# Attention of a diffusion backbone: whole steps, a fused table add and row maximum, and chunks placed between the transposes of the probabilities and their products

## The chip, the cores and the metric

The kernel runs on one core of a Trainium2 chip. The metric is the device time of one execution in microseconds (us). A core has a matrix engine (TensorE, PE in the profile; the loading of its weights is a row of its own, PEld), a vector engine (VectorE, DVE), a scalar engine for functions and copies (ScalarE, ACT), a general engine (GpSimd, POOL) and a queue that issues most transfers (SyncE, SP). Matrix products land in PSUM, eight banks of 128 partitions by 512 numbers of 32 bits; all else lies in SBUF.

## The reference

Two layers over 256 latent tokens of width 1024, with 256 context tokens beside them. Each layer is a half-step gated network, a mixer, and another half-step. The mixer of the first layer is the attention that the change touches:

```python
qkv = (hx @ w_qkv).reshape(B, S, 3, N_HEADS, HEAD_DIM)
q = apply_axial_rope(qkv[:, :, 0], rope)
k = apply_axial_rope(qkv[:, :, 1], rope)
v = qkv[:, :, 2]
...
s_win = jnp.einsum('bjqhd,bjkhd->bhjqk', q_r, k_blk).astype(jnp.float32) * scale
s_win = jnp.where(mask, s_win + bias.astype(jnp.float32)[None], -jnp.inf)
s_ctx = jnp.einsum('bjqhd,bchd->bhjqc', q_r, k_c).astype(jnp.float32) * scale
p = jax.nn.softmax(jnp.concatenate([s_win, s_ctx], axis=-1), axis=-1).astype(v.dtype)
return (jnp.einsum('bhjqk,bjkhd->bjqhd', p[..., :nk], v_blk)
        + jnp.einsum('bhjqc,bchd->bjqhd', p[..., nk:], v_c))
```

The latent tokens are a grid of 4 rows by 64 columns, and there are 16 heads of 64. Every latent query sees all four rows, a window of 16 columns of them with a table of biases per head, and all 256 context keys, in one softmax. So for one head and 128 queries the kernel has a row of 512 scores: 256 latent keys, to which a table of bias and mask is added, and 256 context keys without one.

## The kernel before

All weights stream once from memory. To keep 32-bit accuracy on fast products, every operand is split into a high part (ACT copies it rounded) and a low part (DVE subtracts): `split`, lines 104 to 106, for activations and lines 178 to 181 for weights. One *chunk* is six products of 512 columns (`mmu`, lines 152 to 159).

PE's instructions run in the order in which the code writes them. For the other engines a planner orders the instructions by priority when the kernel is built; `tc.high_priority(offset=n)` moves a group ahead.

Attention is the loop at lines 902 to 930. Before it the first half of the queries (`q_half(0)`) and the first quarter of keys and values (`kv_quarter(0)`) are computed. The rest is a *filler*, which the loop draws chunk by chunk between its own work: `kv_quarter` 1 and 2 (16 chunks each), `q_half(1)` (8 chunks, queries of heads 8 to 15), `kv_quarter(3)` (16 chunks). When it is used up, the output projection (`last_filler`, weights `wo`) follows as filler with nine chunks; its last chunks need the last heads.

A step of two heads and one half `qt` of the queries consists of:

- `scores` (lines 804 to 826): products into two banks S of the PSUM tag "at" (three banks); then per head, on DVE, the table add on the first 256 columns (L818) and the negated row maximum over 512 (L820), on ACT the exponential with its row sum (L822), on DVE the reciprocal (L823), on ACT the scaling (L824);
- `probs_T` (lines 830 to 837) per head: four transposes on PE into a bank of the tag "tp" (two banks), PT, then the split into pT;
- `values` (lines 841 to 861) per head, after both halves of the queries: eight products of 256 columns into a bank of the tag "mm" (three banks), o; ACT copies one half of the partitions (L854), DVE adds the other (L855); every second head is split into oT.

The filler accumulates in "mm" banks too. The projection's order (`order_late`, lines 421 to 427) opens two "mm" banks and then one "at" bank and holds them to the end.

The loop runs over 32 half steps (a head and a query half). Scores of a pair are written at even half steps, one head is transposed two half steps later (A_LAG), its values one more half step later (V_LAG). R0 to R3 say how many chunks are drawn in a half step, half of them before the transposes. The projection starts at half step 24, which is the start of step 12. A piece of work that is due later (`Late`, lines 113 to 125) is written when its count of chunks has passed or when someone needs it: so the transposes of queries (`qT`, line 791) and keys (`kT`, line 773).

The bias table of a head is loaded column-reversed into one of four rotating tiles, POOL adds the mask (L730), and L818 reads it backwards.

Of the kernel before, what the change touches and what calls it, by code (L numbers as in the profile page):

```python
# [20 lines left out]
NH = 16  # L21
# [14 lines left out]
LEAD = 5  # L36
TAIL = 3
XAT = 1
A_LAG = 2
A_PRE = 2  # L40
NX_AT = 2
R0 = 2.4
R1 = 2.9
R2 = 1.9
R3 = 1.0
LN_LAG = (5, 5)
LT_LAG = (5, 5)
F0_LAG = (5, 5, 6, 7)
G_LAG = 4
ROPE_EARLY = 70  # L50
S_EARLY = 40
V_LAG = 1
AHEAD = 3
P_EARLY = 70
V_EARLY = 70
W_HI = 2
# [8 lines left out]
def backbone_kernel(  # L65
# [6 lines left out]
    nc = tc.nc  # L72
# [8 lines left out]
    hp = phase.__enter__()  # L81
# [6 lines left out]
    def nm(s):  # L88
        uid[0] += 1
        return f"{s}_{uid[0]}"  # L90
# [13 lines left out]
    def split(src, hi, lo):  # L104
        nc.scalar.activation(hi, src, AF.Copy)  # L105
        nc.vector.tensor_tensor(out=lo, in0=src, in1=hi.bitcast(F32), op=ALU.subtract)  # L106
# [20 lines left out]
    def settle():  # L127
        while waiting:
            waiting[0].get()
# [72 lines left out]
    warm = cp.tile([1, 1], F32, tag="warm", name="warm")  # L202
    nc.gpsimd.memset(warm, 0.0)
    nc.scalar.activation(warm, warm, AF.Silu)
    crow = cp.tile([16, P], F32, tag="crow", name="crow")
    sync.dma_start(crow[0:8], c[0].rearrange("(a b) -> a b", b=P))
    sync.dma_start(crow[8:16], c_ctx.rearrange("(a b) -> a b", b=P))
    pt = tpb("ctp")
# [172 lines left out]
    def run(gen):  # L381
        for _ in gen:
            pass
# [332 lines left out]
        return r1  # L716

    BIAS = {}

    def bias_pair(h, qt):  # L720


        for hh in (h, h + 1):
            bt = hp.tile([P, 4, 64], F32, tag="bias", bufs=4, name=nm("bias"))
            for i in range(2):
                bias_dma[:] = [sync.dma_start(bt[64 * i:64 * i + 64],
                                              bass.AP(na_rpb_rev.tensor,
                                                      na_rpb_rev.offset + hh * 465 + (7 - 2 * qt - i) * 31 - 48,
                                                      [[1, 64], [31, 4], [1, 64]]))]
            nc.gpsimd.tensor_tensor(out=bt, in0=bt, in1=win_sb[:, ::-1].unsqueeze(1).to_broadcast([P, 4, 64]),  # L730
                                    op=ALU.add)
            BIAS[hh, qt] = bt[:, :, ::-1]

    w_qkv = na_w_qkv[0]

# [16 lines left out]
    def kv_quarter(g, res):  # L752
        krs, v = [], []

        def each(t, bk):
            if t < 2:
                krs.append(roped(bk[:, 0:256], t, 1, 4))
            else:
                r1 = rtile(256)
                nc.scalar.activation(r1, bk[:, 0:256], AF.Copy)  # L760
                krs.append(r1)
            v.append(act(F32R, "v"))
            z = v[t].rearrange("p (h s d) -> p h s d", h=4, s=2)
            split(bk[:, 256:512].rearrange("p (h d) -> p h d", h=4), z[:, :, 0], z[:, :, 1])

        yield from tile_panel(D + g * 256, 2 * D + g * 256, [hTs[t] for t in range(4)], "wkv", each)

        def rest():
            kT = []
            for j in range(2):  # L770
                ps = tpb("kT")
                for t in range(4):
                    nc.tensor.transpose(ps[:, t * P:(t + 1) * P], krs[t][:, j * P:(j + 1) * P], ident)
                hi, lo = act(F32R, "kTh"), act(F32R, "kTl")
                split(ps, hi, lo)
                kT.append((hi, lo))
            return kT

        res.append((Late(1, rest), v))
# [24 lines left out]
    def scores(h, qt):  # L804

        ch = h % 8 // 2
        qh, ql = Q[h // 8].get()[ch // 2]
        qs = slice((ch % 2) * 256 + qt * P, (ch % 2) * 256 + (qt + 1) * P)
        kh, kl = KV[h // 4][0].get()[(h % 4) // 2]
        banks = [bank("at", "S") for _ in range(2)]  # L810
        for f in range(3):
            for i in range(2):
                ps = slice(64 * i, 64 * i + 64)
                nc.tensor.matmul(banks[i], (qh, qh, ql)[f][ps, qs], (kh, kl, kh)[f][ps, :], start=f == 0, stop=f == 2)
        res = []
        for i, S in enumerate(banks):
            Sv = S[:, 0:256].rearrange("p (a b) -> p a b", a=4)
            nc.vector.tensor_tensor(out=Sv, in0=Sv, in1=BIAS.pop((h + i, qt)), op=ALU.add)  # L818
            mx = hp.tile([P, 3], F32, tag="mx", bufs=6, name=nm("mx"))
            nc.vector.tensor_reduce(out=mx[:, 0:1], in_=S, axis=AX.X, op=ALU.max, negate=True)  # L820
            pr = hp.tile([P, 512], F32, tag="pr", bufs=4, name=nm("pr"))
            nc.scalar.activation(pr, S, AF.Exp, bias=mx[:, 0:1], accum_out=mx[:, 1:2])  # L822
            nc.vector.reciprocal(mx[:, 2:3], mx[:, 1:2])  # L823
            nc.scalar.activation(pr, pr, AF.Copy, scale=mx[:, 2:3])  # L824
            res.append(pr)
        return res

    PT = {}
# [57 lines left out]

    box = []
    fill = filler()
    rate = [R0] * 8 + [R1] * 8 + [R2] * 8 + [R3] * 12
    credit = 0.0  # L890
    steps = [(h + i, qt) for h in range(0, NH, 2) for qt in range(2) for i in range(2)]
    prs = {}
    LAG = A_LAG
    fin = None

    def fill_some(n):
        for _ in range(n):
            if next(fill, 0) == 0:
                break

    fill_some(A_PRE)
    for i in range(len(steps) + LAG + V_LAG):
        if i == NX_AT:
            new_x(0, 0, s2t)
            for t in range(2):
# [12 lines left out]
        if i >= 24 and fin is None:  # L918
            run(fill)
            fin = last_filler()  # L920
            fill = islice(fin, 9)
        fill_some((n + 1) // 2)
        if 0 <= i - LAG < len(steps):
            with tc.high_priority(offset=P_EARLY):
                probs_T(*steps[i - LAG], prs.pop(i - LAG))
        fill_some(n // 2)
        j = i - LAG - V_LAG
        if j >= 0 and steps[j][1] == 1:
            with tc.high_priority(offset=V_EARLY):
                values(steps[j][0])  # L930
    run(fill)
    run(fin)
    phase.__exit__(None, None, None)
# [129 lines left out]
```

## Time and profile before

| what | value |
|---|---|
| median of 3 runs | 1285.99 us (1285.16 to 1287.23) |
| profiled execution, its own time | 1289.17 us |
| span of the profiled execution, first to last instruction | 1287.4 us |
| mean granted PE clock | 0.996 |
| first scores of attention (L814) | 441.8 us from the span's start |
| last o product (L849) | 589.2 us |
| DVE over the span | 955.1 us (74%) |
| ACT over the span | 591.2 us (46%) |

The two times differ because one is a single profiled execution and the other the median of runs without a profile. A row of the profile such as `PE o L849 <- DVE pT L106` says that a product of line 849 into the tile o stood idle until the DVE instruction of line 106 had written pT. A PE row shows a product's modelled length; products are pipelined, so the distance from start to start says more about pace.

### The profile page before, as it was taken

The numbers are of one execution on the slowest core, as the hardware profiler recorded it, in microseconds if no ns is written. First come the engines' busy times: TensorE is split into PE (matmuls) and PEld (weight loads), VectorE is DVE, ScalarE is ACT, GpSimd is POOL, SyncE is SP. The second block draws the span as 40 slices with busy tenths as digits, with TensorE's granted clock in tenths as the row PEclk, the third lists the DMA queues.
The fourth block names the chain that finished last, engine by engine and source line by source line (L and its number), as shares of the span: only waits on it lengthen the run. The fifth ranks groups of instructions, "written<-read, shape, count | busy, mean of one in ns | idle before, by whom it ended". The sixth has DMA issues, their size and how long they took to land.

```text
span 1287.4 us, 17193 instructions
## 1 busy us (share of the span) xinstructions
PE 1257.7 (98%) x5890; PEld 1007.0 (78%) x5890; DVE 955.1 (74%) x1683; ACT 591.2 (46%) x1148; POOL 42.0 (3%) x71
## 2 busy tenths in 40 slices
PE   7999999999999999988999999999999999999997
PEld 4787778788778877766887787887787877788886
DVE  3699877485658777788998787757778788855545
ACT  2432132413236456686555435654435645655431
POOL 0000000000001111110000000000000000000000
PEclk9999999999999999999999999999999999999999
DMA  9977569484622744464999887666887764666641
GB/s 284 299 231 243 181 193 297 131 297 146 198 78 76 215 91 92 90 147 149 305 331 328 295 294 262 215 215 225 289 287 241 215 211 147 210 217 185 231 155 51
DMA packets 202712, 268.59 MB, mean 209 GB/s; under 512 B 30026, under 2 KB 149298, under 8 KB 202624
## 3 DMA queue, kind: packets, MB, share of 16 engines
q1 hardware_dynamic: 202624, 267.49, 65.9%
q8 instruction: 46, 0.75, 0.2%
q14 instruction: 42, 0.34, 0.1%
HBM read 265.27 MB, written 2.17 MB: 208 GB/s over the span
## 4 chain that ended last, share of the span: by engine, by line
PE 78%; DVE 8%; DMA 8%; ACT 3%; issue 2%; SPq 1%; POOL 0%; DVEq 0%; ACTq 0%
PE w L156 13%; PE w L157 13%; PE w L159 13%; PE f L541 6%; PE f L542 6%; PE f L543 6%; DMA ar<-in_ada_w_dram 5%; DMA w1r<-in_ffn_w_in_dram 2%; PE wkv L156 2%; PE wkv L157 2%; PE wkv L159 2%; PE wc L156 2%; PE wc L157 2%; PE wc L159 2%; DVE w1l L181 2%
## 5 line engine op out<-in xcount | busy, mean ns | idle before, releaser
L178 ACT ACTIVATE w1h<-w1r 128x512 fp32r<-128x512 f32 x352 | 203.3, 626 | 185.0 <-PE w L159 75.4
L181 DVE TENSOR_TENSOR w1l<-w1r,w1h 128x512 fp32r<-128x512 f32 x352 | 227.6, 684 | 66.5 <-ACT w1h L178 64.3
L156 PE MATMUL w<-w1h,hTh 128*128 128x512 f32 x528 | 211.6, 401 | 3.8 <-ACT hTh L105 3.7
L247 DVE SCALAR_TENSOR_TENSOR acc<-ar,cst,acc 128x512 f32<-128x512 f32 x266 | 187.2, 745 | 34.8 <-DMA ar<-in_ada_w_dram 34.8
L157 PE MATMUL w<-w1l,hTh 128*128 128x512 f32 x528 | 207.7, 393 | 0.0
L156 PE MATMUL w<-w2h,gh 128*128 128x512 f32 (+1 forms) x446 | 175.4, 394 | 0.0
L157 PE MATMUL w<-w2l,gh 128*128 128x512 f32 (+1 forms) x446 | 173.7, 390 | 0.3 <-DVE w2l L181 0.3
L178 ACT ACTIVATE w2h<-w2r 128x512 fp32r<-128x512 f32 x176 | 101.5, 624 | 140.9 <-PE w L159 131.6
L159 PE MATMUL w<-w1h,hTl 128*128 128x512 f32 x528 | 163.9, 392 | 0.6 <-DVE hTl L106 0.6
L181 DVE TENSOR_TENSOR w2l<-w2r,w2h 128x512 fp32r<-128x512 f32 x176 | 114.0, 686 | 43.5 <-ACT w2h L178 42.3
L541 PE MATMUL f<-h0h,w1h 128*128 128x512 f32 x352 | 139.8, 397 | 0.4 <-ACT w1h L178 0.4
L542 PE MATMUL f<-h0h,w1l 128*128 128x512 f32 x352 | 138.4, 393 | 0.0
L543 PE MATMUL f<-h0l,w1h 128*128 128x512 f32 x352 | 138.3, 393 | 0.0
L159 PE MATMUL w<-w2h,gl 128*128 128x512 f32 (+1 forms) x446 | 136.3, 387 | 0.0
L156 PEld LDWEIGHTS w<-w1h,hTh 128*128 128x128 f32 x528 | 99.5, 188 | 28.2 <-ACT hTh L105 5.5
L159 PEld LDWEIGHTS w<-w1h,hTl 128*128 128x128 f32 x528 | 99.5, 189 | 24.1 <-DVE hTl L106 1.4
L157 PEld LDWEIGHTS w<-w1l,hTh 128*128 128x128 f32 x528 | 99.6, 189 | 20.4 <-DVE w1l L181 0.3
L156 PEld LDWEIGHTS w<-w2h,gh 128*128 128x128 f32 x446 | 83.7, 188 | 21.7 <-issue 1.7
L157 PEld LDWEIGHTS w<-w2l,gh 128*128 128x128 f32 x446 | 83.8, 188 | 18.6 <-DVE w2l L181 1.3
L159 PEld LDWEIGHTS w<-w2h,gl 128*128 128x128 f32 x446 | 83.3, 188 | 18.7
L541 PEld LDWEIGHTS f<-h0h,w1h 128*128 128x128 f32 x352 | 66.6, 189 | 18.4 <-issue 3.7
L543 PEld LDWEIGHTS f<-h0l,w1h 128*128 128x128 f32 x352 | 66.5, 189 | 14.7 <-DVE h0l L519 0.3
(178 smaller groups left out, 1702.5 us busy)
## 6 DMA issues: line engine op xcount, KB each, us to landing
w1r<-in_ffn_w_in_dram SPq DMA_DIRECT2D x352, 256.0 KB
ar<-in_ada_w_dram SPq DMA_DIRECT2D x128, 512.0 KB
w2r<-in_ffn_w_out_dram SPq DMA_DIRECT2D x88, 512.0 KB
ar<-in_ada_w_dram SPq DMA_DIRECT2D x32, 256.0 KB
wkvr<-in_na_w_qkv_dram SPq DMA_DIRECT2D x32, 256.0 KB
wcr<-in_sc_w_in_dram SPq DMA_DIRECT2D x32, 256.0 KB
wqr<-in_na_w_qkv_dram SPq DMA_DIRECT2D x8, 512.0 KB
bias<-in_na_rpb_dram SPq DMA_DIRECT2D x64, 64.0 KB
```

The costliest lines, as they stand in the source:

```text
L156: nc.tensor.matmul(ps, lh, rh, start=first and i == 0, stop=False)
L157: nc.tensor.matmul(ps, lh, rl, start=False, stop=False)
L159: nc.tensor.matmul(ps, ll, rh, start=False, stop=last and i == n - 1)
L178: nc.scalar.activation(hi[:, a:a + m // W_HI], raw[:, a:a + m // W_HI], AF.Copy)
L181: nc.vector.tensor_tensor(out=lo[:, a:b], in0=raw[:, a:b], in1=hi[:, a:b].bitcast(F32), op=ALU.subtract)
L247: nc.vector.scalar_tensor_tensor(out=a, in0=src, scalar=sc, in1=a, op0=ALU.mult, op1=ALU.add)
L541: nc.tensor.matmul(ps, lh, hT0[k][0], start=(k == 0), stop=False)
L542: nc.tensor.matmul(ps, ll, hT0[k][0], start=False, stop=False)
L543: nc.tensor.matmul(ps, lh, hT0[k][1], start=False, stop=(k == KC - 1))
```

## The change

The 256-column table add and the 512-column maximum become one DVE instruction over 512 columns: it adds the table, negates, stores the result in place and gives the minimum, which is the negated maximum. For this the table operand has 512 columns too: the head's table and a block of zeros that lies between the tables of the two query halves in one tile of five blocks. The table is no longer read backwards; instead the keys are stored backwards in groups of 64 columns (`back` in the kT split), and the exponential writes its output backwards again. The exponential takes a scale of -1. One reciprocal serves both heads of a step.

The loop runs over 16 whole steps. In step i it writes the scores of step i, half of the step's chunks, both heads' transposes of step i - 1, the other half, and, if that was the second query half, the values of both heads. The chunk counts are per step. The projection starts in step 11, after all work that is due has been written (`settle`). Two small row tiles, `crow` and `srow`, now share the buffers of `mrow`.

```diff
-NX_AT = 2
-R0 = 2.4
-R1 = 2.9
-R2 = 1.9
-R3 = 1.0
+NX_AT = 1
+W_FROM = 11
+R0 = 5.0
+R1 = 4.8
+R2 = 4.0
+R3 = [2, 1, 2, 1, 2]
...
-    crow = cp.tile([16, P], F32, tag="crow", name="crow")
+    crow = sp.tile([32, P], F32, tag="mrow", bufs=2, name="crow")[0:16]
...
+    def back(t):
+
+        return t.rearrange("p (a b) -> p a b", b=64)[:, :, ::-1]
...
+        if not bz:
+            bz.append(hp.tile([P, 5, 4, 64], F32, tag="bias", name="bias"))
+            nc.gpsimd.memset(bz[0][:, 2], 0.0)
         for hh in (h, h + 1):
-            bt = hp.tile([P, 4, 64], F32, tag="bias", bufs=4, name=nm("bias"))
+            n = 3 * qt + hh % 2
+            bt = bz[0][:, n]
...
-            BIAS[hh, qt] = bt[:, :, ::-1]
+            BIAS[hh, qt] = bass.AP(bz[0].tensor, bt.offset, [bt.ap[0], [(2 - n) * 256, 2], [1, 256]])
...
-                split(ps, hi, lo)
+                split(ps.rearrange("p (a b) -> p a b", b=64), back(hi), back(lo))
...
+        mx = hp.tile([P, 6], F32, tag="mx", bufs=4, name=nm("mx"))
         for i, S in enumerate(banks):
-            Sv = S[:, 0:256].rearrange("p (a b) -> p a b", a=4)
-            nc.vector.tensor_tensor(out=Sv, in0=Sv, in1=BIAS.pop((h + i, qt)), op=ALU.add)
-            mx = hp.tile([P, 3], F32, tag="mx", bufs=6, name=nm("mx"))
-            nc.vector.tensor_reduce(out=mx[:, 0:1], in_=S, axis=AX.X, op=ALU.max, negate=True)
+            Sv = S.rearrange("p (c n) -> p c n", c=2)
+            nc.vector.tensor_tensor_reduce(out=Sv, in0=Sv, in1=BIAS.pop((h + i, qt)), scale=-1.0, scalar=3.0e38,
+                                           op0=ALU.add, op1=ALU.min, accum_out=mx[:, i:i + 1])
             pr = hp.tile([P, 512], F32, tag="pr", bufs=4, name=nm("pr"))
-            nc.scalar.activation(pr, S, AF.Exp, bias=mx[:, 0:1], accum_out=mx[:, 1:2])
-            nc.vector.reciprocal(mx[:, 2:3], mx[:, 1:2])
-            nc.scalar.activation(pr, pr, AF.Copy, scale=mx[:, 2:3])
+            nc.scalar.activation(back(pr), S.rearrange("p (a b) -> p a b", b=64), AF.Exp, bias=mx[:, i:i + 1], scale=-1.0,
+                                 accum_out=mx[:, 2 + i:3 + i])
             res.append(pr)
+        nc.vector.reciprocal(mx[:, 4:6], mx[:, 2:4])
+        for i, pr in enumerate(res):
+            nc.scalar.activation(pr, pr, AF.Copy, scale=mx[:, 4 + i:5 + i])
         return res
...
-    rate = [R0] * 8 + [R1] * 8 + [R2] * 8 + [R3] * 12
+    steps = [(h, qt) for h in range(0, NH, 2) for qt in range(2)]
+    rate = [R0] * 4 + [R1] * 4 + [R2] * 3 + [3] + R3
...
-    for i in range(len(steps) + LAG + V_LAG):
+    for i in range(len(steps) + 1):
...
-        while i + AHEAD < len(steps) and len(KV) <= steps[i + AHEAD][0] // 4:
-            fill_some(1)
-        if i < len(steps) and i % 2 == 0:
+        if i < len(steps):
             with tc.high_priority(offset=S_EARLY):
-                prs[i], prs[i + 1] = scores(*steps[i])
-            if i % 2 == 0 and i + 2 < len(steps):
-                bias_pair(*steps[i + 2])
-        credit += rate[min(i, len(rate) - 1)]
+                prs[i] = scores(*steps[i])
+            if i + 1 < len(steps):
+                bias_pair(*steps[i + 1])
+        credit += rate[i]
         n = int(credit)
         credit -= n
-        if i >= 24 and fin is None:
+        fill_some((n + 1) // 2)
+        while i + 1 < len(steps) and len(KV) <= steps[i + 1][0] // 4:
+            fill_some(1)
+        if i:
+            h, qt = steps[i - 1]
+            with tc.high_priority(offset=P_EARLY):
+                for z, pr in enumerate(prs.pop(i - 1)):
+                    probs_T(h + z, qt, pr)
+        if i == W_FROM:
             run(fill)
+            settle()
             fin = last_filler()
             fill = islice(fin, 9)
-        fill_some((n + 1) // 2)
-        if 0 <= i - LAG < len(steps):
-            with tc.high_priority(offset=P_EARLY):
-                probs_T(*steps[i - LAG], prs.pop(i - LAG))
         fill_some(n // 2)
-        j = i - LAG - V_LAG
-        if j >= 0 and steps[j][1] == 1:
+        if i and qt == 1:
             with tc.high_priority(offset=V_EARLY):
-                values(steps[j][0])
+                values(h)
+                values(h + 1)
...
-    srow = cp.tile([24, P], F32, tag="srow", name="srow")
+    srow = sp.tile([32, P], F32, tag="mrow", bufs=2, name="srow")[0:24]
```

More of the change, by code (lines that the diff above doesn't have):

```diff
@@ L38 @@
 XAT = 1
-A_LAG = 2
 A_PRE = 2
-NX_AT = 2
-R0 = 2.4
-R1 = 2.9
-R2 = 1.9
-R3 = 1.0
+NX_AT = 1
[4 more added lines that the diff above has]
+R3 = [2, 1, 2, 1, 2]
 LN_LAG = (5, 5)
@@ L51 @@
 S_EARLY = 40
-V_LAG = 1
-AHEAD = 3
 P_EARLY = 70
@@ L718, in backbone_kernel @@
     BIAS = {}
+    bz = []
+    def back(t):
+        return t.rearrange("p (a b) -> p a b", b=64)[:, :, ::-1]
     def bias_pair(h, qt):
+        if not bz:
+            bz.append(hp.tile([P, 5, 4, 64], F32, tag="bias", name="bias"))
+            nc.gpsimd.memset(bz[0][:, 2], 0.0)
         for hh in (h, h + 1):
-            bt = hp.tile([P, 4, 64], F32, tag="bias", bufs=4, name=nm("bias"))
+            n = 3 * qt + hh % 2
+            bt = bz[0][:, n]
             for i in range(2):
@@ L888, in backbone_kernel @@
     fill = filler()
-    rate = [R0] * 8 + [R1] * 8 + [R2] * 8 + [R3] * 12
+    steps = [(h, qt) for h in range(0, NH, 2) for qt in range(2)]
+    rate = [R0] * 4 + [R1] * 4 + [R2] * 3 + [3] + R3
     credit = 0.0
-    steps = [(h + i, qt) for h in range(0, NH, 2) for qt in range(2) for i in range(2)]
     prs = {}
-    LAG = A_LAG
     fin = None
```

## The prediction, as it was written before the result

> **What bounds the kernel now.** The page comes first. Its first rows say whose time the kernel is.
>
> ```profile
> span 1287.4 us, 17193 instructions
> PE 1257.7 (98%) x5890; PEld 1007.0 (78%) x5890; DVE 955.1 (74%) x1683; ACT 591.2 (46%) x1148; POOL 42.0 (3%) x71
> ```
>
> TensorE (PE) is busy 98% of the span. So an edit that shortens VectorE (DVE) work counts only where PE stands idle for it. The profiled execution took 1289.17 us, 1.8 us more than its span, and 3.2 us more than the 1285.99 us median. I sum against 1289.17 and take 3.2 us off at the end. The change touches attention alone, so the next view is the table by stretches of 10 us over attention (columns: length, then busy us and count of PE, PEld, DVE, ACT and POOL, granted clock, DMA share, GB/s).
>
> ```profile
> 530.00:540.00 10.00, 10.00 (x56) 7.92 (x53) 6.56 (x17) 5.18 (x12) 1.46 (x2) 1.00 0.23 26
> 540.00:550.00 10.00, 8.70 (x52) 6.70 (x50) 7.93 (x17) 9.73 (x23) 2.05 (x2) 1.00 0.43 83
> 550.00:560.00 10.00, 8.04 (x46) 5.71 (x47) 9.51 (x22) 8.85 (x21) 1.47 (x2) 0.89 0.69 104
> 560.00:570.00 10.00, 10.00 (x59) 8.18 (x58) 7.55 (x16) 6.40 (x14) 1.87 (x2) 0.94 0.74 226
> 570.00:580.00 10.00, 9.50 (x57) 7.22 (x56) 8.12 (x19) 9.03 (x20) 3.08 (x4) 1.00 0.48 93
> 580.00:590.00 10.00, 8.04 (x49) 6.33 (x48) 7.30 (x19) 7.00 (x16) 0.00 (x0) 1.00 0.52 157
> ```
>
> Until 540 us PE is full and DVE and ACT have room: there the qkv chunks cover the softmax. From 540 us PE loses 1.30, 1.96, 0.50 and 1.96 us. ACT is at 9.7 of 10 as this begins: the chunks run out before step 11 is over, and the output projection starts only at step 12. The clock row adds a second loss: 0.89 and 0.94 in two stretches are 1.1 + 0.6 = 1.7 us of PE time. Now who ends PE's waits, from the view of waits of PE between 425 and 600 us (total us, times, longest):
>
> ```profile
> PE kT L773 <- DVE pT L106: 2.0, 2, 1.5
> PE o L849 <- DVE pT L106: 1.5, 3, 0.6
> PE o L848 <- DVE osum L855: 0.9, 1, 0.9
> PE wo L156 <- ACT oT L105: 0.9, 1, 0.9
> PE o L848 <- ACT pT L105: 0.7, 1, 0.7
> PE PT L836 <- DVE pT L106: 0.5, 1, 0.5
> ```
>
> That is 6.5 us. And where each sits, from the timeline (start, length, idle before it in brackets):
>
> ```profile
> 549.02 0.39 PE L848 MATMUL o<-pT,v 128*128 128x256 f32 x1 [0.74 <-ACT pT L105]
> 549.97 0.39 PE L849 MATMUL o<-pT,v 128*128 128x256 f32 x1 [0.56 <-DVE pT L106]
> 556.55 0.66 PE L773 MATMUL kT<-ident,kr 128*128 128x128 f32 x4 [1.55 <-DVE pT L106]
> 575.69 0.38 PE L849 MATMUL o<-pT,v 128*128 128x256 f32 x1 [0.50 <-DVE pT L106]
> 585.03 0.66 PE L836 MATMUL PT<-ident,pr 128*128 128x128 f32 x4 [0.54 <-DVE pT L106]
> 588.24 0.38 PE L848 MATMUL o<-pT,v 128*128 128x256 f32 x1 [0.92 <-DVE osum L855]
> 589.30 0.40 PE L156 MATMUL wo<-woh,oT 128*128 128x512 f32 x1
> ```
>
> The reader is to see that no row names the table add or the maximum. PE waits for probabilities that were transposed too recently (o behind PT), for a transpose bank (kT behind PT), and once, at 588.24, for the only free bank of o.
>
> **The change part by part.** Prices first, from the view of groups with shapes apart (count, busy us, mean ns, idle before).
>
> ```profile
> L818 DVE TENSOR_TENSOR S<-S,bias 128x256 f32<-128x256 f32 x32 | 12.6, 422 | 4.2 <-PE S L814 3.2 <-issue 0.6
> L820 DVE TENSOR_REDUCE mx<-S 128x1 f32<-128x512 f32 x32 | 20.7, 677 | 0.1
> L823 DVE RECIPROCAL mx<-mx 128x1 f32<-128x1 f32 x32 | 5.1, 158 | 4.9 <-ACT pr L822 4.8
> L106 DVE TENSOR_TENSOR pT<-PT,pT 128x512 fp32r<-128x512 f32 x32 | 21.9, 687 | 11.9 <-ACT pT L105 11.4
> L247 DVE SCALAR_TENSOR_TENSOR acc<-ar,cst,acc 128x512 f32<-128x512 f32 x266 | 187.2, 745 | 34.8 <-DMA ar<-in_ada_w_dram 34.8
> L822 ACT ACTIVATE pr<-S,mx 128x512 f32<-128x512 f32 x32 | 21.9, 689 | 18.8 <-DVE mx L820 18.7
> L822 ACT ACTIVATION_READ_ACCUMULATOR pr<-S,mx 128x1 f32 x32 | 6.4, 201 | 0.0
> L824 ACT ACTIVATE pr<-pr,mx 128x512 f32<-128x512 f32 x32 | 22.6, 726 | 0.5 <-DVE mx L823 0.5
> L105 ACT ACTIVATE pT<-PT 128x512 fp32r<-128x512 f32 x32 | 18.9, 595 | 11.3 <-PE PT L836 11.2
> L708 DVE TENSOR_TENSOR qr<-wq,rope 128x512 f32<-128x512 f32 x4 | 2.7, 682 | 0.0
> L713 DVE TENSOR_TENSOR r<-wq,rope 128x256 f32<-128x256 f32 x8 | 3.0, 412 | 0.0
> L715 DVE TENSOR_TENSOR qr<-qr,r 128x512 f32<-128x512 f32 x4 | 2.7, 681 | 0.0
> L855 DVE TENSOR_TENSOR osum<-o,osum 64x256 f32<-64x256 f32 x16 | 6.6, 416 | 4.8 <-ACT osum L854 4.6
> L253 POOL MEMSET adab<- 128x512 f32 x2 | 1.1, 543 | 0.5 <-PE wo L159 0.5
> ```
>
> *DVE.* A pair of heads costs now 2 x (0.42 + 0.68 + 0.16) = 2.52 us. The fused instruction is not in this trace. From below, the two-input instruction over 512 columns with one input in PSUM: 0.69. From above, twice that, 1.38. Its extra output of one number per partition costs something between nothing and ACT's 0.20; one 128x1 DVE instruction takes 0.16. I take 0.69 + 0.16 = 0.85, so a pair costs 2 x 0.85 + 0.16 = 1.86, and 16 pairs save 16 x 0.66 = 10.6 us of DVE. Behind PE's 10.00 rows that is worth nothing. Late, it brings the maxima earlier: the first at 0.85 instead of 1.5 us behind the scores, the second at 1.7 instead of 2.2. [...]
>
> *ACT.* The count stays, and the order becomes Exp, Exp, Copy, Copy: the first Copy now waits for the second Exp (0.89) and the common reciprocal. Exp and the kT split write 64-column groups backwards. L818 reads its table backwards at 422 ns, as L855 takes 416 for 256 columns without it; a backward write is not shown. Bounds: nothing, and 0.13 us (the spread of ACT's 512-column copies, 595 to 726 ns); I take nothing.
>
> *The order on PE* is where the time is decided, since PE runs in written order. Block lengths from the chain of waits:
>
> ```profile
> 446.72 0.45 PE wkv L159 x2
> 448.53 0.90 PE S L814 x6
> 450.56 0.46 PE wkv L159 x2
> 451.92 0.46 PE wkv L159 x2
> 453.73 0.46 PE wkv L159 x2
> ```
>
> A chunk is 451.92 - 450.56 = 1.36 us, a PT block between two chunks 453.73 - 451.92 - 1.36 = 0.45, scores 450.56 - 448.53 - 0.90 = 1.13 (0.90 is the chunk's part ahead of its last two matmuls). An o block is 589.30 - 588.24 = 1.06. Merging blocks changes these sums by nothing I can read. So the result is waits gone against waits new.
>
> Gone. (a) Chunks last longer. Drawn are 2 ahead of the loop, 20 in steps 0 to 3, 19 in steps 4 to 7, 12 in steps 8 to 10; three of the 56 are left for step 11, where the projection also begins. The waits at 549 us, 0.74 + 0.56, go. (b) 0.50 at 575.69 goes. (c) The slow clock behind that cluster, 1.7, goes if no cluster like it comes back. Together 3.5 us.
>
> Kept. kT behind two PT blocks at step 11: the settle call puts it right behind both transposes, where PE again waits for both banks (about 1.8, now 2.0). The last o (0.92) and the last projection (0.9).
>
> New. (d) Queries of heads 8 to 15. Their eight chunks are draws 33 to 40, and step 8 begins after draw 41. Now they are transposed long before their use; then only one chunk, 1.36 us, lies between the last query chunk and scores that need it. The rotation takes DVE 0.68 + 2 x 0.41 + 0.68 = 2.18 us, with half a 0.69 instruction ahead of it 2.5; PE waits 2.5 - 1.36 = 1.2, then 0.4 for the first split (ACT 0.60 and signals against 0.45 of the second half's transposes), and 0.4 for the low part: 2.0. Behind them on PE stand the scores and chunks of step 8, so all of PE waits. Bounds 0.8 (DVE free, low part covered) and 3.5 (two instructions ahead). (e) From step 12 the projection holds two of three banks of tag mm. Both values blocks of a pair now follow one another at steps 12, 14 and 16, so the second waits for the copy and add of the first, as at 588.24: 0.92 each, two more than now, 1.85. What is queued behind it on PE is the next scores. (f) Steps with one chunk (13 and 15). From the scores' end to their PT: chunk, two PT, scores, chunk = 1.36 + 0.90 + 1.13 + 1.36 = 4.75 at step 13, without the scores 3.6 at step 15. Needed: 0.85 + 2 x 0.89 + 0.16 + 0.73, an allowance of 0.5 for the signals between engines, and ACT's two pT copies (1.19) that fall in between: 5.2. PE waits 0.5 and 1.6; now the same place has 0.54 and, behind it, 0.42 (the third of the L849 waits): 1.1 more. Bounds 0 and 3, as ACT also splits projection weights there.
>
> Sum: -3.5 + 2.0 + 1.85 + 1.1 - 0.2 (kT) = +1.25 us, so 1289.17 + 1.25 - 3.2 = 1287.2 us. The rest lies beside full PE rows and is costed at nothing: the memset of the zero block on POOL (half the columns of L253's 0.54 us; uncovered, at most that, once), the row buffers shared in place of own ones, and the SP queue, which issues the same four bias loads per step; the projection's loads of rows and residual now follow the bias loads of step 12, a step earlier than now.
>
> **The rivals.** *Faster.* If DVE starts the rotation at once and ACT keeps up, (d) falls to 0.8 and (f) to nothing, and kT, with the projection's work spread out, to half: 1.25 - 1.2 - 1.1 - 1.0 = -2.05; with the backlog of weight splits worked off earlier the last two waits (1.8) halve: about -3, 1283 us. For it: ACT has room before 540. Against: the two bank waits are fixed by the order. *Slower by the clock.* The granted clock fell once, behind the two kT waits: 2.0 us idle of the 3.2 from 553.9 to 557.1. (d) is 2 us idle around 0.9 us of transposes, and kT 1.8: if each draws it down as there, twice 1.7, less nothing: 1287.2 + 3.4 = 1290.6. It decides once the idle is as dense as at 556.55; at the tail (585 to 589), less dense, the clock stayed at 1.00. *Slower by the fused instruction.* At 1.38 it delays both maxima of a pair; behind (f) that is 2 x 0.53 per step, twice, less some cover: +1.6, 1288.8. [...] *The change does not do what it says:* the DVE work saved was never waited for. That holds in the forecast too; alone, without new waits, it is 1286.
>
> **How the numbers follow.** Within 0.2% (2.6 us, about what a measurement of this kernel can tell): the forecast, and the saving that nobody feels, 0.44. Faster by more: 0.22. Slower by more: the clock 0.18, the fused instruction 0.08, both (f) and (d) at their upper ends (+3.4) 0.08, together 0.34. The range leaves out a tenth on each side: low, the faster rival with 0.5 us to spare, 1282.5; high, the clock's case, 1291.
>
> **What would show it.** Right: a PE wait of 1 to 3 us at the qT transposes; three o waits near 0.9 for osum, two steps apart; kT waiting for pT as before; no wait at o before step 11; DVE's attention work about 10 us less with no PE row changed before 500 us. Wrong: no wait at qT, a fused instruction over 1 us, Exp above 0.75 us, or a granted clock below 1.00 behind step 8.

## The result and the profile after

| kernel | median us | lowest to highest | runs | ratio, 95% interval |
|---|---|---|---|---|
| before | 1285.99 | 1284.13 to 1290.62 | 7 | 1 |
| changed | 1293.38 | 1290.03 to 1297.05 | 7 | 1.0058 [1.0041, 1.0075] |

The change makes the kernel 7.4 us slower by the medians. The forecast was 1287.2, and the range ended at 1291. Of all executions in this document, one of q_early_o_apart (3216.62 us) and one of before beside it (1391.09 us) were slow ones, which the medians hold and the ratios leave out. The profiled execution of the changed kernel took 1290.03 us, the fastest of its seven, and that of before 1289.17 us, one of its slower ones. Side by side the two totals hide most of the difference, so the reading starts with the page and then cuts attention out of both.

```profile
span 1288.2 us, 17176 instructions
PE 1255.6 (97%) x5890; PEld 1005.7 (78%) x5890; DVE 945.2 (73%) x1667; ACT 591.1 (46%) x1148; POOL 42.0 (3%) x72
```

DVE has lost 9.9 us (955.1 before) and 16 instructions, and the span has not followed. The timeline of PE gives the two ends of attention: the first scores, and the first transpose of the next network, gT. First before, then after (start, length, line):

```profile
441.83 0.50 PE L814 MATMUL S<-kTh,qTh 64*128 64x512 f32 x2
623.07 0.60 PE L400 MATMUL gT<-ident,sil 128*128 128x128 f32 x4
```

```profile
440.83 0.51 PE L821 MATMUL S<-kTh,qTh 64*128 64x512 f32 x2
629.22 0.60 PE L398 MATMUL gT<-ident,sil 128*128 128x128 f32 x4
```

That is 181.2 us before and 188.4 after: attention is 7.2 us longer, about as much as the medians differ. The profiled before was longer elsewhere: by 1.0 us ahead of the first scores, for which these rows show no cause, and by 5.4 us behind attention. There PE's waits have this row in before, and after this one:

```profile
PE w L156 <- ACT hTh L105: 3.3, 2, 2.7
```

```profile
PE w L154 <- ACT hTh L103: 0.8, 2, 0.6
```

With a stretch of slow clock behind the wait of 2.7 (at 800 us, shown below), that is 2.5 + 1.7 = 4.2 of the 5.4 us, in code that the change does not touch.

Now the changed attention, from the view of PE's waits between 425 and 625 us (total, times, longest):

```profile
PE o L857 <- DVE osum L864: 4.1, 3, 1.7
PE PT L845 <- DVE kTl L104: 2.3, 2, 1.7
PE kT L780 <- DVE pT L104: 2.0, 2, 1.4
PE qT L798 <- DVE qr L713: 1.6, 1, 1.6
...
PE PT L845 <- DVE pT L104: 0.9, 2, 0.5
...
PE S L821 <- DVE qTl L104: 0.4, 1, 0.4
PE S L821 <- ACT qTh L103: 0.3, 1, 0.3
```

All rows of this view together are 14.0 us; the same view of before adds up to 8.1. None of the waits of products o for probabilities (1.5 and 0.7 before) is left. Two rows have grown, o for its bank (0.9 before) and PT behind kTl (0.2 before), and the queries are new. The timeline of PE shows where they sit:

```profile
500.02 1.15 PE L780 MATMUL kT<-ident,kr 128*128 128x128 f32 x8
...
504.29 0.66 PE L845 MATMUL PT<-ident,pr 128*128 128x128 f32 x4 [1.74 <-DVE kTl L104]
...
521.31 0.98 PE L798 MATMUL qT<-ident,qr 128*128 128x128 f32 x7 [1.56 <-DVE qr L713]
...
581.33 0.38 PE L857 MATMUL o<-pT,v 128*128 128x256 f32 x1 [1.74 <-DVE osum L864]
...
594.28 0.38 PE L857 MATMUL o<-pT,v 128*128 128x256 f32 x1 [1.45 <-DVE osum L864]
```

At 500.02 the key transposes take both banks of tag "tp" (x8: two blocks of four). One chunk later, PT of step 6 wants the same two banks, and the split of kT has not emptied them. The timelines of ACT and DVE show why one chunk is too little. ACT scaled the probabilities of both heads (1.34 us) before it came to kT, DVE stood 1.01 us for that half of the split, and between the two banks DVE had a weight split.

```profile
501.68 1.34 ACT L834 ACTIVATE pr<-pr,mx 128x512 f32<-128x512 f32 x2
502.90 0.61 ACT L103 ACTIVATE kTh<-kT 128x512 fp32r<-128x512 f32 x1
...
503.54 0.69 DVE L104 TENSOR_TENSOR kTl<-kT,kTh 128x512 fp32r<-128x512 f32 x1 [1.01 <-ACT kTh L103]
504.15 0.68 DVE L179 TENSOR_TENSOR wkvl<-wkvr,wkvh 128x512 fp32r<-128x512 f32 x1
504.75 0.68 DVE L104 TENSOR_TENSOR kTl<-kT,kTh 128x512 fp32r<-128x512 f32 x1
```

The last o shows the same for the bank of tag "mm". Its release is a copy of 0.38 us on ACT and an add of 0.41 on DVE, but both engines were in the middle of a pair of weight splits of the projection:

```profile
591.94 1.15 ACT L176 ACTIVATE woh<-wor 128x512 fp32r<-128x512 f32 x2 [0.78 <-PE wo L157]
592.60 1.29 DVE L179 TENSOR_TENSOR wol<-wor,woh 128x512 fp32r<-128x512 f32 x2 [0.72 <-ACT woh L176]
593.11 0.38 ACT L863 ACTIVATE osum<-o 64x256 f32<-64x256 f32 x1
593.81 0.41 DVE L864 TENSOR_TENSOR osum<-o,osum 64x256 f32<-64x256 f32 x1
```

The longest wait, at 581.33, has another cause. The o that it waits for ended at 579.6, and ACT did this first, so that its copy began at 580.44:

```profile
579.67 0.75 ACT L834 ACTIVATE pr<-pr,mx 128x512 f32<-128x512 f32 x1
```

The other loss is clock. In stretches of 3.4 us (columns as in the table by stretches: length, PE busy, ..., granted clock, DMA share, GB/s) after shows two of them at half clock in attention, each behind a stretch in which PE was busy about half of the time:

```profile
520.30:523.70 3.40, 1.77 (x13) 1.10 (x13) 3.40 (x6) 1.22 (x3) 0.81 (x1) 1.00 0.63 203
523.70:527.10 3.40, 3.40 (x9) 2.38 (x10) 3.04 (x8) 1.45 (x4) 0.00 (x0) 0.50 0.56 156
...
578.30:581.70 3.40, 1.60 (x12) 1.26 (x11) 2.54 (x6) 3.38 (x8) 0.89 (x2) 1.00 0.11 19
581.70:585.10 3.40, 3.40 (x16) 2.37 (x15) 1.39 (x3) 1.05 (x3) 0.00 (x0) 0.50 0.73 237
```

Before has one in attention, and the one at 800 us:

```profile
554.30:557.70 3.40, 1.80 (x12) 1.18 (x14) 3.00 (x8) 3.37 (x9) 0.74 (x1) 1.00 0.92 190
557.70:561.10 3.40, 3.40 (x10) 2.26 (x11) 3.40 (x7) 1.25 (x3) 0.93 (x2) 0.50 0.41 58
...
800.10:803.50 3.40, 3.40 (x10) 2.62 (x9) 3.30 (x7) 3.40 (x7) 0.00 (x0) 0.50 0.11 35
```

At a clock of 0.50 a slow stretch of 3.4 us is taken to cost half of it, 1.7 us. That is an estimate: in the one at 523.70 the products of a chunk start 0.43 us apart, and 0.23 at 530 us, which would make it 1.6. So attention is longer by 14.0 - 8.1 = 5.9 us of waits and one more slow stretch, 1.7: 7.6 against the 7.2 measured between its ends. The extra slow stretch is not a chance of these two executions alone: the mean granted clock over the change's seven runs is 0.995, and 0.996 to 0.997 over the runs of before beside the experiments. That is 0.0014 to 0.0017 of 1288 us, about 2 us.

Last the parts of the softmax, from the view of groups with shapes apart (count, busy us, mean ns, idle before):

```profile
L826 DVE CUSTOM_DVE_ANT_1 S<-S,bias 128x512 f32<-128x512 f32 x24 | 16.6, 695 | 7.5 <-PE S L821 5.0 <-POOL bias L737 1.8 <-issue 0.4
L826 DVE DVE_READ_ACCUMULATOR2_ANT mx<- 128x1 f32 x32 | 4.1, 127 | 0.2
L829 ACT ACTIVATE pr<-S,mx 128x512 f32<-128x512 f32 x32 | 21.9, 686 | 22.0 <-DVE mx L826 21.8 <-DVE gcol L297 0.2
```

The fused instruction takes 695 + 127 ns = 0.82 us (eight of the 32 took 725), where 0.85 was forecast. Writing backwards costs ACT nothing (686 ns, 689 before), and DVE's split of the keys with reversed groups takes 0.69 and 0.68 us in the rows at 503.54 and 504.75, what a split without it takes (687 ns for pT before).

### The profile page after: what moved, and what is told of

Read it like the earlier page. It is cut to its first block, busy times and chain, and to the rows that moved or that the text cites. A ratio compares the mean times of both kernels' runs of the same rounds, so it can differ in the third digit from the quotient of the medians.

```text
span 1288.2 us, 17176 instructions
## 1 busy us (share of the span) xinstructions
PE 1255.6 (97%) x5890; PEld 1005.7 (78%) x5890; DVE 945.2 (73%) x1667; ACT 591.1 (46%) x1148; POOL 42.0 (3%) x72
## 4 chain that ended last, share of the span: by engine, by line
PE 87%; DVE 4%; DMA 4%; ACT 3%; issue 1%; SPq 0%; POOL 0%; DVEq 0%; ACTq 0%
PE w L154 16%; PE w L155 16%; PE w L157 16%; PE f L539 6%; PE f L541 6%; PE f L540 6%; DMA ar<-in_ada_w_dram 2%; PE wkv L154 2%; PE wkv L155 2%; PE wkv L157 2%; PE wc L154 2%; PE wc L155 2%; PE wc L157 2%; DMA w1r<-in_ffn_w_in_dram 1%; PE gT L398 1%; PE S L821 1%
## 5 line engine op out<-in xcount | busy, mean ns | idle before, releaser
L245 DVE SCALAR_TENSOR_TENSOR acc<-ar,cst,acc 128x512 f32<-128x512 f32 x266 | 187.2, 745 | 30.9 <-DMA ar<-in_ada_w_dram 30.6
```

The source lines that it names most:

```text
L245: nc.vector.scalar_tensor_tensor(out=a, in0=src, scalar=sc, in1=a, op0=ALU.mult, op1=ALU.add)
```

## The experiments

All were timed in five rounds beside the kernel before, whose median was 1286.62, 1286.95 and 1286.20 us in the three jobs. Ratios are to the kernel before of the same job. A gain "against the change" is the difference of two ratios to before, times 1286 us, since the kernels ran in different jobs.

| kernel | median us (runs) | ratio to before, 95% | against the change, us | attention, us | PE's waits in it, us | slow stretches in it |
|---|---|---|---|---|---|---|
| before | | 1 | -7.5 | 181.2 | 8.1 | 1 |
| changed | 1293.38 (7) | 1.0058 [1.0041, 1.0075] | 0 | 188.4 | 14.0 | 2 |
| fused_alone | 1285.80 (12) | 0.9995 [0.9980, 1.0009] | -8.1 | 181.9 | 8.2 | 1 |
| loop_alone | 1292.08 (6) | 1.0046 [1.0031, 1.0061] | -1.5 | 187.8 | 13.0 | 2 |
| q_early | 1286.27 (12) | 1.0012 [0.9997, 1.0027] | -5.9 | 182.0 | 9.3 | 1 |
| o_apart | 1289.28 (12) | 1.0026 [1.0011, 1.0040] | -4.1 | 183.3 | 10.4 | 1 |
| q_early_o_apart | 1286.16 (12) | 0.9997 [0.9984, 1.0010] | -7.8 | 181.3 | 8.4 | 1 |
| kT_two_chunks | 1290.84 (12) | 1.0039 [1.0025, 1.0053] | -2.4 | 187.2 | 12.7 | 2 |
| pe_kept_busy | 1291.93 (8) | 1.0047 [1.0031, 1.0062] | -1.4 | 190.2 | 12.8 | 3 |
| pe_kept_busy_3 | 1290.47 (11) | 1.0031 [1.0019, 1.0043] | -3.5 | 186.4 | 9.9 | 0 |
| all_apart_cover | 1284.86 (12) | 0.9988 [0.9975, 1.0000] | -9.0 | 180.3 | 8.6 | 1 |
| tuned | 1282.03 (10) | 0.9970 [0.9954, 0.9985] | -11.3 | 178.4 | 7.9 | 0 |

The last three columns come from the one profiled execution of each kernel: the time from the first scores to the first gT, the sum of PE's waits in it, and the number of stretches of 3.4 us at half clock. Taking off the waits, 1.7 us for each slow stretch, and in the pe_kept_busy kernels the work that they add, leaves 170.0 to 172.0 us in all twelve. So waits and clock account for the differences between these kernels' attention to about 1 us.

### Which half of the change costs: fused_alone and loop_alone

fused_alone is the kernel before with its half-step loop, and of the change only the softmax: the fused instruction, the block of zeros, the reversed writes, the common reciprocal and the shared row tiles. loop_alone is the opposite: the changed loop with the old softmax. Both compute all of the reference.

```diff
# loop_alone, against the changed kernel
-            nc.vector.tensor_tensor_reduce(out=Sv, in0=Sv, in1=BIAS.pop((h + i, qt)), scale=-1.0, scalar=3.0e38,
-                                           op0=ALU.add, op1=ALU.min, accum_out=mx[:, i:i + 1])
+            nc.vector.tensor_tensor(out=Sv, in0=Sv, in1=BIAS.pop((h + i, qt)), op=ALU.add)
+            nc.vector.tensor_reduce(out=mx[:, 0:1], in_=S, axis=AX.X, op=ALU.max, negate=True)
...
-                split(ps.rearrange("p (a b) -> p a b", b=64), back(hi), back(lo))
+                split(ps, hi, lo)
```

> The fused instruction, the backward writes and the common reciprocal alone, in the loop of before. Theory (the order on TensorE loses the time; the fused instruction is neither waited for nor slow): the same as before within 0.2%, 1283 to 1289 us; the fused instruction at about 0.70 us and its readout at 0.13, about 10 us of VectorE work less, and the waits at o and kT from 549 to 557 us still there. Rival (the fused softmax loses the time, since the first scaling now waits for the second exponential): slower by 4 to 7 us, with new waits of TensorE for PT or o.

> The new loop with the table add, the maximum and two reciprocals as before. Theory: slower than before by 6 to 9 us, like the change, with the wait at qT (1.6 us), at PT behind kT (2.3 us in total) and three waits at o for osum. Rival (the fused softmax is the cost): within 2 us of before.

fused_alone runs as before runs, although its page shows the whole saving on DVE:

```profile
PE 1254.5 (98%) x5890; PEld 1004.7 (78%) x5890; DVE 945.2 (74%) x1667; ACT 591.2 (46%) x1148; POOL 42.0 (3%) x72
```

9.9 us of DVE work are gone, and the time lies between 0.2% below and 0.1% above that of before. loop_alone has the loss, 5.9 us against before where at least 6 was expected, and its waits of PE are in kind those of the change:

```profile
PE o L846 <- DVE osum L853: 4.3, 3, 1.7
PE qT L789 <- DVE qr L713: 2.3, 1, 2.3
...
PE PT L834 <- DVE kTl L104: 0.9, 1, 0.9
```

So the loss is the order of the loop and not the fused instruction. What loop_alone lacks of the loss (1.5 us, with intervals that overlap) can be the shorter wait at PT (0.9 for 2.3). With the old softmax ACT split the first kT ahead of the two scalings and not behind them. Its qT wait is longer (2.3 for 1.6), and this pair does not settle the share.

### The queries one step earlier: q_early

The chunks per step become 5.5 (steps 0 to 3), 4.8 and then 4, 3, 3, so that two more chunks are drawn early. The draws of the four key transposes and of qT move against the steps.

```diff
-R0 = 5.0
+R0 = 5.5
-R2 = 4.0
+R2 = [4, 3, 3]
```

> The changed kernel with two chunks more drawn in steps 0 to 3 and two fewer in steps 9 and 10, so that two chunks lie between the last query chunk and the qT transposes, and three between the key transposes of heads 8 to 11 and the next PT. Theory: no wait at qT, none at PT for kT, and no lower granted clock behind step 8: 2.3 + 1.6 + 0.7 us of waits and about 2 us of slow clock go, so 5 to 7 us less than the changed kernel, 1286 to 1289 us. Rival (these waits only move the loss to later steps, where ScalarE sets the pace): less than 2 us gained, with the o and PT waits of steps 12 to 16 longer by as much.

```profile
PE o L857 <- DVE osum L864: 4.2, 3, 1.8
...
PE qT L798 <- DVE pT L104: 0.4, 1, 0.4
```

The wait for the rotation (1.6, with 0.7 behind it) and the wait of PT for kTl (2.3) have gone. All rows of the view now add up to 9.3 us, 4.7 less than in the change, and the time fell by about 5.9. The rest is less than one slow stretch (1.7), and the profile has one in attention where the change has two; one execution does not tell how often. The waits for osum stay as they were.

### The two values blocks apart: o_apart, and both together

In o_apart the values of a pair's second head are written after the next step's scores and first chunks, in place of right behind the first head's.

```diff
+    late_o = []
...
+        while late_o:
+            with tc.high_priority(offset=V_EARLY):
+                values(late_o.pop())
         if i:
...
                 values(h)
-                values(h + 1)
+            late_o.append(h + 1)
```

> The changed kernel with the values of the second head of a pair written after the first chunks of the next step, not right behind those of the first head. Theory: two of the three o waits for osum go (4.1 us in total now, 1.5 left at the end), so 2 to 3.5 us less than the changed kernel, 1290 to 1292 us. Rival (ScalarE sets the pace of steps 12 to 16, and PE waits elsewhere instead): less than 1 us gained, with PT or o waits for pT longer by as much.

> Both moves together: draws two chunks earlier in steps 0 to 3, and the second head's values behind the next step's first chunks. Theory (the waits at qT, at PT behind kT and at o are separate losses, each with its share of slow clock): the gains add up, 8 to 11 us less than the changed kernel, so 1282.5 to 1285.5 us, 1 to 4 us under the kernel before; of the waits only kT behind PT (2 us), the last o (1.4) and the projection's first wait (0.9) are left. Rival (ScalarE's work in steps 11 to 16 sets a floor that each move alone has nearly reached): no better than the better of the two alone, 1286 us.

In o_apart only the last o has a neighbour, and only it waits:

```profile
PE o L857 <- DVE osum L864: 1.4, 1, 1.4
```

That is 2.7 us of bank waits gone. All rows add up to 10.4 us, 3.6 less than in the change, and the time fell by 4.1, a little more than was expected; the profile has one slow stretch less. The two edits together gave 7.8 and not 5.9 + 4.1: the expected sum of the gains did not come. What one frees, the next bank takes. In the joint kernel qT waits for a "tp" bank that pT still holds, twice, and kT waits longer than in q_early:

```profile
PE kT L780 <- DVE pT L104: 2.5, 3, 1.8
...
PE qT L798 <- DVE pT L104: 1.2, 2, 0.8
```

The median is where the rival put it, but its cause, a floor that ScalarE sets at about 1286 us, does not hold: tuned, below, runs at 1282.03 with the same softmax.

### One chunk or two between kT and PT: kT_two_chunks

The only edit is in step 6: four chunks ahead of the transposes of the probabilities and one behind them, in place of three and two. Then two chunks lie between kT and PT.

```diff
-        fill_some((n + 1) // 2)
+        fill_some(4 if i == 6 else (n + 1) // 2)
...
-        fill_some(n // 2)
+        fill_some(1 if i == 6 else n // 2)
```

> The changed kernel with four chunks ahead of the transposes of step 6 and one behind, in place of three and two; nothing else moves. So two chunks lie between the key transposes of heads 8 to 11 and the PT transposes that use the same two banks. Theory: the wait of PT for the kT split in step 6 (1.7 + 0.5 us) falls below 0.3 us and 1.5 to 2.3 us are gained, 1290.5 to 1292 us; the wait at qT stays at 1.6 or grows by some tenths. Rival (that wait is covered by another one behind it): less than 0.7 us gained.

```profile
PE PT L845 <- DVE kTl L104: 0.9, 2, 0.5
```

The longest of these waits falls from 1.7 to 0.5 us: 1.2 us, about the 1.36 of a chunk. The sum falls from 2.3 to 0.9, and the time by 2.4 (the intervals of the two ratios overlap). The wait was expected to fall below 0.3, which it did not. So the wait that the prediction lacked is in the main a matter of distance on PE.

### Is the clock a cost of its own: pe_kept_busy and pe_kept_busy_3

These add work. pe_kept_busy writes seven more products of 512 columns into the bank of qT ahead of its transposes, which overwrite them; pe_kept_busy_3 also writes seven into a bank of "mm" ahead of PT in step 6 and six ahead of the settle call, read by nobody. PE is then busy where it would have waited.

```diff
+                if g == 1 and j == 0:
+                    kk = KV[1][0].get()[1][0]
+                    for _ in range(7):
+                        nc.tensor.matmul(ps, kk[:, 0:P], kk, start=True, stop=True)
```

> The changed kernel with seven products of no use (1.6 us of TensorE work, their result is overwritten) ahead of the qT transposes, where TensorE waits 1.6 us for the rotation. Nothing that the rotation needs waits for them. Theory (the lower granted clock behind step 8 is drawn down by the idle time): the granted clock between 510 and 535 us stays at 1.00 and the 1.5 to 2 us of slow chunks behind the scores go, so 1 to 2 us less than the changed kernel although it does more work. Rival (the slow clock there has another cause, or falls by chance): the clock falls there as before, and the time is that of the changed kernel or up to 0.5 us more.

> The changed kernel with products of no use at three of its waits: seven ahead of the qT transposes, seven ahead of the PT transposes of step 6, six ahead of the last kT (1.6, 1.6 and 1.4 us of TensorE work). Theory (idle time draws the granted clock down, whichever of the waits falls into one stretch of the clock's control): no clock below 1.00 from 490 to 575 us; 2 to 3 us less than the changed kernel, 1290 to 1291.5 us, in spite of the added work; what is left is at the o waits. Rival (the slow clock is not drawn by these waits, or costs little): the time of the changed kernel, 1293, or more by the added work that delays something.

With the first block alone the stretch behind qT is fast, and one behind an o is slow as in the change (0.83 from 580 to 590 us in both), but two further stretches are slow which were fast in the profile of the change. From the table by stretches, first pe_kept_busy, then the change:

```profile
500.00:510.00 10.00, 7.72 (x35) 5.96 (x34) 5.24 (x11) 5.95 (x14) 1.08 (x2) 0.83 0.72 161
...
520.00:530.00 10.00, 9.37 (x50) 7.05 (x49) 8.61 (x18) 6.04 (x13) 1.47 (x2) 1.00 0.59 168
...
560.00:570.00 10.00, 9.16 (x44) 7.13 (x44) 6.70 (x14) 5.89 (x13) 1.01 (x2) 0.84 0.83 272
```

```profile
500.00:510.00 10.00, 7.72 (x46) 6.25 (x45) 6.09 (x12) 5.85 (x14) 1.48 (x2) 1.00 0.71 154
...
560.00:570.00 10.00, 9.08 (x56) 7.09 (x56) 6.21 (x13) 5.66 (x13) 0.73 (x1) 1.00 0.83 259
```

PE's busy time from 500 to 510 us is 7.72 in both, and the clock 0.83 and 1.00. So gaps of the same sum went with a lower clock in one execution and not in the other, and this kernel alone could not decide. With three gaps filled, pe_kept_busy_3 shows a clock of 1.00 in every such stretch from 500 to 600 us, also the one that holds the slow stretch of the change behind an o. Nothing was filled there, and its waits for osum (4.2 us) stay, so that this place was fast by the chance of one execution:

```profile
580.00:590.00 10.00, 9.32 (x55) 7.29 (x56) 6.44 (x17) 6.83 (x15) 0.00 (x0) 1.00 0.34 105
```

Its mean clock is 0.995 to 0.999 in its eleven runs against 0.993 to 0.996 in the seven of the change, and it is 3.5 us faster with 20 more products. A product is a sixth of a chunk, 1.36 / 6 = 0.23 us, so they take 4.5 us; the waits in the view fall from 14.0 to 9.9, by 4.1. By these two the kernel would be 0.4 us slower. What it gained agrees with the clock: averaged over the executions of each kernel, the granted clock rose from 0.9949 to 0.9973, and 0.0024 of 1288 us is 3.1 us. So in these runs idle time of PE cost clock beyond itself. The size is known poorly: it is a difference of two ratios, each known to some 0.15%, so 3.5 us with an uncertainty of 2.7.

### All at once: all_apart_cover and tuned

all_apart_cover takes q_early and o_apart, starts the projection ahead of the transposes in step 11 without the settle call, gives the last o a bank of tag "at" and writes one of the projection's last chunks earlier, right behind the last o. tuned keeps the projection's order as it was, and has the chunks of each step written out, before and behind the transposes:

```diff
+PRE = [3, 3, 2, 3, 3, 2, 3, 1, 2, 2, 2, 1, 0, 1, 1, 1, 1]
+POST = [3, 2, 4, 2, 2, 3, 2, 4, 2, 1, 1, 2, 1, 0, 1, 0, 1]
...
-        fill_some((n + 1) // 2)
+        fill_some(PRE[i])
...
+        fill_some(2 if i == W_FROM else 0)
         if i == W_FROM:
             run(fill)
-            settle()
...
-        fill_some(n // 2)
+        fill_some(POST[i])
...
+    with tc.high_priority(offset=V_EARLY):
+        values(late_o.pop(), 1)
```

The second argument of `values` names the "at" bank; `late_o` is that of o_apart.

> Both moves, and three more: the projection's first two chunks around the last kT transposes and ahead of PT of step 10, the last o in a bank of tag at instead of mm, and one chunk of the projection's last bank between the last o and the chunks that need the last heads. Theory: the waits at kT (2.0), the last o (1.4) and the projection (0.9) go as well, 3 to 4.5 us on top of the two moves, 1279 to 1282 us, under the kernel before by 0.3 to 0.5%. Rival (by then ScalarE, which splits weights and probabilities in steps 11 to 16, ends every wait): 0 to 1.5 us on top, with PT waiting for pr or pT instead.

> The two moves (chunks earlier, values of the second head apart) with the counts of chunks ahead of and behind PT written out per step, so that two chunks lie between PT and every kT or qT in the same banks, and behind kT or qT ahead of their use; the transposes of step 10 go ahead of the last kT; the last o takes a bank of tag at. Theory (each wait on TensorE is a matter of distance, in chunks, between a block and the one that frees its bank or makes its operand): kT, qT and PT wait under 0.5 us each up to step 11, no o waits for osum, and 0.9 (the projection) and about 1 at PT of step 15 remain; 1281 to 1284 us, under the kernel before by 0.2 to 0.4%. Rival (ScalarE's floor in steps 11 to 16): as the two moves alone, 1285 to 1287 us, with the waits at PT and o for pr and pT longer.

all_apart_cover missed its expectation. The o waits for osum have gone, and others took their place:

```profile
PE w L154 <- ACT hTh L103: 2.0, 1, 2.0
PE qT L798 <- DVE pT L104: 1.3, 2, 0.7
```

The first of them (0.7 in the change) is put down to the moved chunk, which had covered the layer norm behind attention. tuned gives that chunk back and has 1.0 there in two pieces, but it changes other things too. It also spaces the "tp" blocks, and it beats both kernels, before by 0.3% [0.15%, 0.46%]. Its top row of waits, and a row of its table by stretches:

```profile
PE PT L846 <- DVE pT L105: 1.7, 3, 1.0
```

```profile
580.00:590.00 10.00, 8.36 (x47) 6.58 (x46) 7.14 (x13) 4.83 (x10) 0.00 (x0) 1.00 0.22 69
```

No row of its waits names osum, and none has a single wait over 1.0 us. That kT, qT and PT would wait under 0.5 us up to step 11 was expected and did not come: qT waited up to 0.9 us. The time fell into the range expected. PE is idle for 1.64 us between 580 and 590 and the clock stays at 1.00, where the change had a slow stretch. Its waits add up to 7.9 us, hardly less than the 8.1 of before; what differs more is the clock, 0.997 to 0.999 in its ten runs against 0.992 to 0.999 in the 21 of before beside it. How much of its gain over before is the fused instruction was not tried: that would need the same order with the old softmax.

## Why the prediction was wrong

The prediction summed to +1.25 us; attention became 7.2 us longer. By its own terms, forecast against measured:

| term | forecast | measured |
|---|---|---|
| DVE saving | 0 | 0 (fused_alone) |
| (a), (b), (f): o waiting for probabilities, and PT | -0.74 - 0.56 - 0.50 + 1.1 = -0.7 | 1.5 + 0.7 + 0.5 became 0.9: -1.8 |
| kT at step 11 | -0.2 | 2.0 before, 2.0 after: 0 |
| (d) the queries | +2.0 | 1.6 + 0.4 + 0.3 = +2.3 |
| (e) bank of o | +1.85 | 0.9 became 4.1: +3.2 |
| PT behind kT in step 6 | not in the list | 0.2 became 2.3: +2.1 |
| (c) clock | -1.7 | +1.7 |

The right column adds up to 7.5, 0.3 us more than the two ends of attention give. It exceeds the forecast by 6.3 us, of which the clock is 3.4, the unlisted wait 2.1 and (e) 1.4.

- **Right: what the DVE saving is worth.** "Behind PE's 10.00 rows that is worth nothing" was the first claim, and fused_alone shows it. The rival by which the fused instruction takes 1.38 us fell with 0.82 measured. No run shows the 1.38: it was the author's estimate, twice the 0.69 of a two-input instruction over 512 columns, and the fused one took 695 ns and 127 for its readout.
- **Right: (d) and kT.** The queries wait, and by nearly what was forecast (2.5 - 1.36 is 1.1 and not 1.2, which changes little). kT was forecast to stay and stayed.
- **Wrong, but small: (f).** It was to be PT waiting for probabilities that are not ready. No row of the change has PT waiting for pr. What PT waits for, 0.9 in all, is pT, that is a "tp" bank, and so was the 0.54 of before that (f) took for the same thing. No run shows the 0.5 us that (f) allows for signals; in the rows of kTl above, DVE starts 0.03 us behind the end of ACT's split (503.51 and 503.54).
- **Mis-sized: (e).** All three waits came where they were forecast, as DVE's osum and two steps apart. The price was one row, 0.92, taken three times. The first, at 568.43, took that; the other two took 1.74 and 1.45. The release passes through ACT and DVE. Ahead of it ACT had a scaling of probabilities (0.75 us) at 581, and at 593 both engines were in the projection's weight splits (1.15 and 1.29 us). The prediction counted such work of ACT in (f) and did not carry it over to (e). o_apart shows the term to be real.
- **Failed: the list of new waits.** Under "New" the prediction went through the queries, o and the tail. It applied the rule of the two "tp" banks at step 11 alone. The new count of chunks also moved a kT block to one chunk ahead of PT in step 6, and 2.1 us of wait were missed. kT_two_chunks takes away 1.4 of them with one chunk more between.
- **Failed: the clock.** Step (c) took 1.7 us off "if no cluster like it comes back", while the same text put two such clusters into the new order, (d) and kT. In the profile the stretch behind kT was fast (1.00 from 550 to 570 us), but the ones behind (d) and behind an o were slow (0.50 from 523.70 and from 581.73 us). That was the rival "slower by the clock", at a chance of 0.18 and 1290.6 us; pe_kept_busy_3 supports it. The forecast should have kept the 1.7 at least, since PE's waits in the new order were not smaller than in the old (14.0 and 8.1 us).

The range was too narrow at its upper end for the same reason as the forecast: it took the clock's case alone, and not with an upper end of (e) or one unlisted wait beside it.

## What to carry to other kernels

Where one engine runs in written order, a re-ordering is priced per block: for each, count what lies between it and the block that frees its bank or makes its operand, at every place where the pattern occurs, and take the release at the length it has behind whatever fills the releasing engines there. A saving on an engine that the bottleneck does not wait for was worth nothing by itself here (fused_alone: 9.9 us less on DVE, 0.9995 of the time), and waits that are removed uncover others on the same few banks, so the gains of single edits did not add up (q_early_o_apart: 7.8 us, and not 5.9 + 4.1). In these runs idle time of the matrix engine that lay close together could cost more than itself, by the estimate 1.7 us of clock each time, so filling it was worth something (pe_kept_busy_3: 3.5 us, with an uncertainty of 2.7). That spreading the same waits thinly is worth as much fits tuned, but was not tried by itself.

## What the runs showed of the hardware

Every slow stretch in the profiles of before and after, up to the last product, is a clock of 0.50 for 3.41 us: from 557.73 and 800.08 us in before, from 523.70 and 581.73 in after. Within each of the two executions the starts lie a whole number of such stretches apart: 242.35 us = 71 x 3.413 in before, and 58.03 = 17 x 3.413 in after. In the three cases in attention the 3.40 us ahead had PE busy for 1.60 to 1.80 us, so 1.60 to 1.80 us of idle time, in pieces of at most 1.74; ahead of the one at 800 us PE was busy for 0.69.

The reverse does not hold. In after PE was busy for 1.77 us both from 503.20 to 506.60 us, around PT in step 6, and from 520.30 to 523.70, and the clock of the next 3.4 us was 1.00 behind the first and 0.50 behind the second. In pe_kept_busy the clock from 500 to 510 us was 0.83, with PE busy for the same 7.72 us as in after. That it matters how much of a cluster of gaps falls into one such stretch is the author's estimate; these runs do not settle it.

The clock explains a part of the scatter of 7 us among the change's runs. The run of 1297.05 us has a clock of 0.993 and that of 1290.03 has 0.996, and 0.003 of 1290 us is 3.9 us. The rest stays open.
